# Up projection of a hybrid encoder layer: one matmul of 512 columns in place of two of 256, and sums of products kept in PSUM

## The chip, the cores and the metric

The kernel runs on one core of a Trainium2 chip. The metric is the time of one execution in microseconds; the comparison is by the median of several runs.

## What is computed

One layer of a bidirectional encoder on a sequence of 512 tokens with 2048 channels, in float32. Cut to what matters here:

```python
xn = rms_norm(x, attn_norm_g)
u_val, u_gate, q, k, v = split(xn @ w_in)            # 2048 -> 5120
y_conv = conformer_conv(u_val, u_gate, ...)          # width 31, layer norm, swish
y_na = neighborhood_attention(q, k, v, rpb)          # 16 heads, 8 x 64 grid
x = x + concat(rms_norm(y_conv), rms_norm(y_na)) @ w_out
xn = rms_norm(x, ffn_norm_g)
up = depthwise_conv(xn @ w_up, ffn_dw_w, ffn_dw_b)   # 2048 -> 11264, width 3
gate, val = split(up)
x = x + (silu(gate) * val) @ w_down                  # 5632 -> 2048
return rms_norm(x, final_norm_g)
```

## The kernel before

Every large matrix is used in two parts, so that matmuls in a fast float32 format give nearly full precision: a high part (`whi`, the value rounded to the format, made by ScalarE) and a low part (`wlo`, the rest, made by VectorE as a difference). A product is then three matmuls: high weights by high data, high weights by low data, low weights by high data (`mm3`, L126 to L128).

The stages follow one another: the input projection `project` (80 units of 8 x 3 matmuls of 512 columns, with convolution and attention beside it), the output projection `out_half` (two halves of 16 units), the up projection `up` and `hidden` (44 blocks f, each of 128 gate and 128 value columns), and the down projection (`product2`). The up and the down projection use a scheme for 2 x 2 blocks with seven products in place of eight, numbered c = 0 to 6. The weights of a product are a quarter of the matrix's block (A11, A12, A21, A22) or a sum of quarters: c = 0, 3 and 5 take A22, A11 and A12 as they are; c = 1 is A22 + A21, c = 2 is A21 + A11, c = 4 is the sum of 1 with A11, c = 6 the sum of 4 with A12. Signs are put into the data. `TURN` and `TURN2` are the orders of the products in the two projections.

Data of a product in the up projection: `comb[c][k]`, a tile of 128 x 512, whose left half holds the high parts of 256 combined token columns and whose right half the low parts.

Weights come by one list, `plan`: `weights()` takes the next entry, and has the entries up to 3 ahead (`AHEAD`) made. An entry made means: a load of 512 KB from HBM into one of seven `raw` buffers (`raw_unit`, on SyncE's queue, L110), then the split into `whi` and `wlo` (`parts`, L115 and L116), of which there are four buffers each. Sums of quarters begin earlier, up to 8 entries ahead (`FAR`), by the table `sums`. In the up projection the sums 1 and 2 are a load and a second transfer, on POOL's queue, that adds to the buffer (`summed`, L588); 4 and 6 are made by VectorE in the buffer of 1 (L595). For the down projection the sums are made in HBM ahead of time: a job copies a quarter to a scratch tensor `wsum[c][k]` (L176) and a second transfer adds another quarter to it (L177). There are 4 x 22 jobs. `sum_ahead` issues one behind a given matmul; it is called after certain units of the input and output projections, and after the fourth product of each block of the up projection.

The order of work on each engine is made by a scheduler from the order of the program and the dependencies; each engine then executes its own queue in that order, and POOL's and SyncE's queues issue the transfers. Of PSUM's eight banks, three have the tag "mm", one "po", two together "sc", and two "tr".

In a block of the up projection the products 3, 0, 1, 4, 5, 2, 6 go into four PSUM tiles of 256 columns. Products 4 and then 2 are added onto product 3, and product 6 onto product 1. ScalarE keeps copies in between (`kept`, L641), and VectorE adds (L648 to L650):

```python
a = kept(uu[:, 0], product(3))
kept(vv[:, 0], product(0))
b = kept(vv[:, 1], product(1))
kept(uu[:, 1], product(4, a))
add(g[:, 0], uu[:, 0], product(5))
add(v, vv, both(product(2, a)))
add(g[:, 1], uu[:, 1], product(6, b))
```

The rest of `hidden` scales, runs the width-3 convolution (L658 to L660), silu and the product with the gate, and writes the hidden row to HBM (the last 8 stay).

Of the kernel before, what the change touches and what calls it, by code (L numbers as in the profile page):

```python
# [10 lines left out]
F32 = mybir.dt.float32  # L11
F32R = mybir.dt.float32r
AF = mybir.ActivationFunctionType
ALU = mybir.AluOpType
# [20 lines left out]
U = 8  # L35
# [12 lines left out]
NW = 4  # L48
NEG = -1.0e30

TURN = (3, 0, 1, 4, 5, 2, 6)
TURN2 = (3, 0, 4, 1, 2, 6, 5)
Q = D // 2 // S
TAIL = 4
# [16 lines left out]
def layer(ctx: ExitStack, tc: tile.TileContext, xT, w_in, w_out, w_up, w_down, par, tab, g3, out):  # L71
# [36 lines left out]
    def raw_unit(src, n):  # L108
        raw = t4([P, U * P], "raw")
        return raw, nc.sync.dma_start(raw[:, :n], src)  # L110

    def parts(raw, n):
        hi = wpool.tile([P, U * P], F32R, tag="whi", name="whi", bufs=NW)
        lo = wpool.tile([P, U * P], F32R, tag="wlo", name="wlo", bufs=NW)
        i = nc.scalar.activation(hi[:, :n], raw[:, :n], AF.Copy)  # L115
        j = nc.vector.tensor_sub(lo[:, :n], raw[:, :n], hi[:, :n].bitcast(F32))  # L116
        return hi, lo, i, j

    def unit(src, n):

        return parts(raw_unit(src, n)[0], n)[:2]
# [37 lines left out]


    A11, A12, A21, A22 = range(4)
    wsum = {c: [dram.tile([P, U * P], F32, name=f"ws{c}_{k}") for k in range(NK)] for c in (1, 2, 4, 6)}
# [7 lines left out]
    def sum_ahead(ins):  # L170

        if not jobs:
            return
        c, k = jobs.pop(0)
        a, b = {1: (w_down[k, A22], A21), 2: (w_down[k, A21], A11), 4: (wsum[1][k], A11), 6: (wsum[4][k], A12)}[c]
        behind(nc.gpsimd.dma_start(wsum[c][k], a), ins)  # L176
        nc.gpsimd.dma_start(wsum[c][k], w_down[k, b], accum_op=ALU.add, max_dma_last_dim=ROW)  # L177

# [7 lines left out]
    def sum_sq(acc, src, first, to=slice(0, S)):  # L186
        if first:
            nc.scalar.activation(acc, src, AF.Square)
        else:
            q = t2("sq")[:, to]  # L190
            nc.scalar.activation(q, src, AF.Square)
            nc.vector.tensor_add(acc, acc, q)

    def rsqrt_steps(acc, n, name, to=slice(0, S), keep=True):

        m = (to.stop - to.start) // P
        ps = psa.tile([P, 2, S], F32, tag="sc", name="st")[:, 0]
# [16 lines left out]
        ps = psa.tile([P, 2, S], F32, tag="sc", name="st")[:, 0]  # L214
# [4 lines left out]
        nc.scalar.activation(res[:, to], ps[:, :m * P], AF.Copy)  # L219
        return res  # L220
# [51 lines left out]
    def project(n):  # L272
        ps = psm.tile([P, S], F32, tag="mm", name="pj")
        for u in range(KD // U):
            w = weights()
            for k in range(U):
                kk = u * U + k
                m = mm3(ps, w, k, xs[kk][0], xs[kk][1], kk == 0, kk == KD - 1)
            tick(m)
            if weights.at > 6 and weights.at % 2:  # L280
                sum_ahead(m)
            while late:
                late.pop()()
        return ps
# [292 lines left out]
    def stats2():  # L577
        rstd2.append((yield from rsqrt_steps(acc2, D, "rstd2")))

    def factors(f, at):  # L580

        def load(q):
            a[q] = raw_unit(w_up[f, q], U * P)[0]
            return a[q]

        def summed(c, q1, q2):
            a[c] = raw_unit(w_up[f, q1], U * P)[0]
            nc.gpsimd.dma_start(a[c], w_up[f, q2], accum_op=ALU.add)  # L588

        def make(c):  # L590
            if c in plain:
                return load(plain[c])
            if c in (1, 2):
                return a["s%d" % c]
            add(a["s1"], a["s1"], a[A11 if c == 4 else A12])  # L595
# [11 lines left out]
    order2 = [*range(NK - KEEP // 2, NK), *range(NK - KEEP // 2)]  # L607
    for c in TURN2:
        for k in order2:
            plan.append(lambda c=c, k=k: (unit(wsum[c][k] if c in wsum else w_down[k, {0: A22, 3: A11, 5: A12}[c]],  # L610
                                               U * P), operand(c, k)))

    out_half(mb, after)
    steps.append(stats2())

    def up(f, done):

        def product(c, onto=None):

            w = weights()  # L620
            ps = onto
            if ps is None:
                ps = (psa.tile([P, S], F32, tag="po", name="pu") if c == 1 else
                      psm.tile([P, S], F32, tag="mm", name="pu"))[:, :H]
            for k in range(U):
                m = comb[c][k]
# [3 lines left out]
            return ps  # L630

        def pair(name):
            return t2(name).rearrange("p (i t) -> p i t", i=2)

        def both(x):
            return x.unsqueeze(1).broadcast_to([P, 2, H])

        vv, uu, v, g = pair("vv"), pair("uu"), pair("vl"), pair("g")

        def kept(t, ps):  # L640
            nc.scalar.activation(t, ps, AF.Copy)  # L641
            return ps

        a = kept(uu[:, 0], product(3))
        kept(vv[:, 0], product(0))
        b = kept(vv[:, 1], product(1))
        kept(uu[:, 1], product(4, a))
        add(g[:, 0], uu[:, 0], product(5))  # L648
        add(v, vv, both(product(2, a)))
        add(g[:, 1], uu[:, 1], product(6, b))  # L650
        g, v = (t.rearrange("p i t -> p (i t)") for t in (g, v))
        return g, v

    def conv3(a, n):
# [24 lines left out]
    def operand(c, k):  # L679

        (b11, b12), (b21, b22) = ((hs[i][:, :H], hs[i][:, H:]) for i in (2 * k, 2 * k + 1))
        if c in (3, 5, 6):
            src = {3: b11, 5: b21, 6: b22}[c]
        else:
            t = t2("hc")
            src, m = t[:, :H], t[:, H:]
            if c == 2:
                nc.vector.tensor_sub(src, b22, b12)
            elif c == 1:
                nc.vector.tensor_sub(src, b11, b12)  # L690
# [7 lines left out]
        nc.vector.tensor_sub(t[:, H:], src, t[:, :H].bitcast(F32))  # L698
        return t
# [213 lines left out]
```

## Time and profile before

| | |
|---|---|
| time, median of 3 runs (lowest, highest) | 2038.44 us (2036.22, 2039.22) |
| the profiled execution's own time | 2037.69 us |
| its span | 2035.9 us |
| mean granted TensorE clock | 0.997 |
| TensorE matmuls, busy | 2005.8 us |
| VectorE, busy | 1593.5 us |
| ScalarE, busy | 1017.6 us |
| HBM read, written | 425.02 MB, 110.10 MB |

The span is from the first to the last instruction of one profiled execution. Matmuls are pipelined, so the duration of one (283 ns for 256 columns in the up projection) is longer than the step from one to the next. By the matmuls on each line, the input projection and the attention end near 505 us, the output projection near 708, the up projection runs from 708.1 to 1599.3, and the down projection from there to the end. DMA shares are the mean busy share of the 16 DMA engines; q1 carries the transfers issued by SyncE, q0 those issued by POOL.

### The profile page before, as it was taken

How to read it: one execution, taken by the hardware profiler on the slowest of the kernel's cores; microseconds unless marked ns; L12 is line 12 of the kernel's file. 1: busy time of each engine (PE TensorE's matmuls, PEld its weight loads, DVE VectorE, ACT ScalarE, POOL GpSimd, SP SyncE). 2: the span in 40 equal slices, each digit the busy share in tenths (PEclk: the TensorE clock that was granted, in tenths of full speed). 3: DMA queues.
4: the chain of work that ended last, by engine and by line, in shares of the span. 5: the costliest groups of instructions: out<-in, count | busy, mean ns of one | idle time of the engine just before them, and what ended most of it. 6: DMA issues, size and time to landing. Idle time of an engine off the chain costs nothing.

```text
span 2035.9 us, 32324 instructions
## 1 busy us (share of the span) xinstructions
PE 2005.8 (99%) x12620; PEld 1795.3 (88%) x12620; DVE 1593.5 (78%) x2223; ACT 1017.6 (50%) x1548; POOL 227.7 (11%) x314
## 2 busy tenths in 40 slices
PE   8999999999999999999999999999999999999997
PEld 6888888877787899999999999999999888888886
DVE  7985798497547878888888888888888698885764
ACT  6234423447525654545455555555455544554663
POOL 0111111011001111111111111111110300000000
PEclk9999999999999999999999999999999999999999
DMA  6676677677757889999999999999886976666563
GB/s 234 167 224 182 171 177 202 181 185 207 227 145 202 206 215 257 239 255 244 252 245 247 258 247 248 245 255 245 237 222 181 341 233 217 213 213 195 191 213 124
DMA packets 140873, 444.96 MB, mean 219 GB/s; under 512 B 15793, under 2 KB 23985, under 8 KB 139313
## 3 DMA queue, kind: packets, MB, share of 16 engines
q1 hardware_dynamic: 97776, 292.94, 42.5%
q0 software_dynamic: 42944, 149.97, 35.3%
q8 instruction: 99, 1.62, 0.3%
q14 instruction: 54, 0.43, 0.1%
HBM read 425.02 MB, written 110.10 MB: 263 GB/s over the span
## 4 chain that ended last, share of the span: by engine, by line
PE 76%; issue 21%; ACT 1%; DMA 1%; DVE 1%; POOL 0%; SPq 0%; POOLq 0%; DVEq 0%
PE pu L126 15%; PE pu L127 15%; PE pu L128 15%; PE pj L126 7%; PE pj L128 6%; PE pj L127 6%; PE po L126 3%; PE po L127 3%; PE po L128 3%; PE po L437 1%; PE sc L397 1%; PE trp L424 1%; DMA raw<-in_w_in 1%; DMA tab<-in_tab 0%; PE trx L537 0%
## 5 line engine op out<-in xcount | busy, mean ns | idle before, releaser
L115 ACT ACTIVATE whi<-raw 128x1024 fp32r<-128x1024 f32 x574 | 606.2, 1057 | 810.7 <-PE pj L127 219.3
L116 DVE TENSOR_TENSOR wlo<-raw,whi 128x1024 fp32r<-128x1024 f32 x574 | 700.7, 1222 | 265.2 <-ACT whi L115 230.4
L126 PE MATMUL pu<-xc,whi 128*128 128x256 f32 x2464 | 697.5, 283 | 1.3 <-ACT uu L641 1.3
L128 PE MATMUL pu<-xc,wlo 128*128 128x256 f32 x2464 | 697.9, 283 | 0.0
L127 PE MATMUL pu<-xc,whi 128*128 128x256 f32 x2464 | 697.7, 283 | 0.0
L126 PEld LDWEIGHTS pu<-xc,whi 128*128 128x128 f32 x2464 | 473.1, 192 | 2.0 <-ACT uu L641 1.7
L128 PEld LDWEIGHTS pu<-xc,wlo 128*128 128x128 f32 x2464 | 473.1, 192 | 0.2 <-issue 0.2
L127 PEld LDWEIGHTS pu<-xc,whi 128*128 128x128 f32 x2464 | 473.2, 192 | 0.1
L126 PE MATMUL pj<-xh,whi 128*128 128x512 f32 x640 | 254.0, 398 | 7.7 <-ACT whi L115 7.7
L128 PE MATMUL pj<-xh,wlo 128*128 128x512 f32 x640 | 251.0, 392 | 1.1 <-DVE wlo L116 1.1
L127 PE MATMUL pj<-xl,whi 128*128 128x512 f32 x640 | 251.3, 393 | 0.0
L737 PE MATMUL pd<-whi,ho 128*128 128x512 f32 x616 | 240.5, 391 | 2.2 <-DVE ho L698 2.2
L735 PE MATMUL pd<-whi,ho 128*128 128x512 f32 x616 | 240.5, 391 | 1.3 <-ACT ho L697 1.3
L736 PE MATMUL pd<-wlo,ho 128*128 128x512 f32 x616 | 240.6, 391 | 0.0
L311 DVE SCALAR_TENSOR_TENSOR y<-ch,prm,y 128x507 f32<-128x507 f32 (+14 forms) x240 | 169.7, 738 | 3.3
L126 PEld LDWEIGHTS pj<-xh,whi 128*128 128x128 f32 x640 | 120.8, 189 | 35.8 <-ACT whi L115 9.0
L128 PEld LDWEIGHTS pj<-xh,wlo 128*128 128x128 f32 x640 | 120.8, 189 | 28.6 <-DVE wlo L116 2.5
L127 PEld LDWEIGHTS pj<-xl,whi 128*128 128x128 f32 x640 | 120.9, 189 | 24.7 <-issue 0.7
L737 PEld LDWEIGHTS pd<-whi,ho 128*128 128x128 f32 x616 | 116.1, 188 | 27.1 <-DVE ho L698 3.0
L735 PEld LDWEIGHTS pd<-whi,ho 128*128 128x128 f32 x616 | 115.9, 188 | 25.7 <-ACT ho L697 1.5
L736 PEld LDWEIGHTS pd<-wlo,ho 128*128 128x128 f32 x616 | 116.0, 188 | 24.9 <-DVE wlo L116 0.6
L177 POOL DMA_DIRECT2D ws<-in_w_down x88 | 79.5, 904 | 360.5 <-DMA ws<-ws 185.1
(161 smaller groups left out, 2029.1 us busy)
## 6 DMA issues: line engine op xcount, KB each, us to landing
raw<-in_w_up SPq DMA_DIRECT2D x220, 512.0 KB, 5.8
ws<-in_w_down POOLq DMA_DIRECT2D x132, 512.0 KB, 7.3
raw<-in_w_up POOLq DMA_DIRECT2D x88, 512.0 KB, 7.9
raw<-ws SPq DMA_DIRECT2D x88, 512.0 KB, 4.2
raw<-in_w_in SPq DMA_DIRECT2D x80, 512.0 KB, 4.8
raw<-in_w_down SPq DMA_DIRECT2D x66, 512.0 KB, 4.0
ws<-ws POOLq DMA_DIRECT2D x44, 512.0 KB, 4.7
raw<-in_w_out SPq DMA_DIRECT2D x32, 512.0 KB, 4.7
```

Of the source, the lines that this page charges most:

```text
L115: i = nc.scalar.activation(hi[:, :n], raw[:, :n], AF.Copy)
L116: j = nc.vector.tensor_sub(lo[:, :n], raw[:, :n], hi[:, :n].bitcast(F32))
L126: nc.tensor.matmul(ps, hi[:, a], mh, start=start, stop=False, skip_group_check=more)
L127: nc.tensor.matmul(ps, hi[:, a], ml, start=False, stop=False, skip_group_check=more)
L128: return nc.tensor.matmul(ps, lo[:, a], mh, start=False, stop=stop, skip_group_check=more)
L177: nc.gpsimd.dma_start(wsum[c][k], w_down[k, b], accum_op=ALU.add, max_dma_last_dim=ROW)
L311: nc.vector.scalar_tensor_tensor(y[:, a:b], h[:, a + j - PAD:b + j - PAD], prm[:, o + j:o + j + 1], y[:, a:b], op0=ALU.mult, op1=ALU.add)
L397: m = nc.tensor.matmul(both[:, j, i, :], q[hp, b * P:(b + 1) * P], grid(k, KC0[b], KW)[hp], start=True, stop=True)
L424: m = nc.tensor.transpose(ps[:, 2 * i + ch, :], s[:, i, ch * P:(ch + 1) * P], ident)
L735: nc.tensor.matmul(ps[i], h[:, t], wh[:, d], start=start and not more, stop=False, skip_group_check=more)
L736: nc.tensor.matmul(ps[i], h[:, t], wl[:, d], start=False, stop=False, skip_group_check=more)
L737: return nc.tensor.matmul(ps[i], h[:, tl], wh[:, d], start=False, stop=stop, skip_group_check=more)
```

## The change

The up projection computes both products with the high weights by one matmul: high weights by the whole tile of 512 columns, whose left half is by the high data and whose right half by the low. The low weights follow by a matmul of 256 columns into the left half. A product thus fills a whole PSUM bank, and its value is the sum of the two halves; `folded` makes it (ScalarE copies the right half, VectorE adds the left). Where a product must be added to a sum that another product needs as well, ScalarE copies the bank into a second bank (`copied`), and the matmuls go on adding there. Three matmuls ahead of the up projection write the banks once. Six banks are held for the whole stage; the statistics use a "tr" bank there.

The weights of c = 4 get a `raw` buffer of their own (VectorE adds 1 and A11 into it), and after their split a transfer on POOL's queue adds A12 to it for c = 6. For the down projection the sums for c = 2 are no longer made in HBM: each is loaded and added to in a `raw` buffer, up to 8 entries ahead of its use. There remain 3 x 22 jobs, called at other units. The order of the products in a block becomes 3, 2, 4, 5, 1, 0, 6.

```diff
-TURN = (3, 0, 1, 4, 5, 2, 6)
+TURN = (3, 2, 4, 5, 1, 0, 6)
...
-    wsum = {... for c in (1, 2, 4, 6)}
-    jobs = [(c, k) for k in range(NK) for c in (1, 4, 2, 6)]
+    wsum = {... for c in (1, 4, 6)}
+    jobs = [(c, k) for k in range(NK) for c in (1, 4, 6)]
...
+    def stat():
+        if where:
+            return psa.tile([P, S], F32, tag="tr", name="st", bufs=2)
+        return psa.tile([P, 2, S], F32, tag="sc", name="st")[:, 0]
...
-            if weights.at > 6 and weights.at % 2:
+            if weights.at > 6 and weights.at % 3:
                 sum_ahead(m)
...
-            if d % 3 == 0:
+            if d % 2:
                 sum_ahead(i)
...
         def make(c):
             if c in plain:
                 return load(plain[c])
-            if c in (1, 2):
-                return a["s%d" % c]
-            add(a["s1"], a["s1"], a[A11 if c == 4 else A12])
-            return a["s1"]
+            if c == 4:
+                a[4] = t4([P, U * P], "ws")
+                add(a[4], a[1], a["q", A11])
+            return a[4 if c == 6 else c]
+
+        def split_of(c):
+            w = parts(make(c), U * P)[:2]
+            if c == 4:
+                nc.gpsimd.dma_start(a[4], w_up[f, A12], accum_op=ALU.add)
+            return w
...
-        for c, qs in ((1, (A22, A21)), (2, (A21, A11))):
-            sums[at + TURN.index(c)] = lambda c=c, qs=qs: summed("s%d" % c, *qs)
-        return [lambda c=c: parts(make(c), U * P)[:2] for c in TURN]
+        sums[at + TURN.index(2)] = lambda: summed(2, A21, A11)
+        sums[at + TURN.index(4)] = lambda: summed(1, A22, A21)
+        return [lambda c=c: split_of(c) for c in TURN]
...
+    def summed2(k):
+        third[k] = raw_unit(w_down[k, A21], U * P)[0]
+        nc.gpsimd.dma_start(third[k], w_down[k, A11], accum_op=ALU.add)
+
+    def unit2(c, k):
+        if c == 2:
+            return parts(third[k], U * P)[:2]
+        return unit(...)
+
     for c in TURN2:
         for k in order2:
+            if c == 2:
+                sums[len(plan)] = lambda k=k: summed2(k)
...
+    ea = psa.tile([P, 2, S], F32, tag="sc", name="pu")
+    pd_, pb, pc_ = (psm.tile([P, S], F32, tag="mm", name="pu") for _ in range(3))
+    pe, pa = ea[:, 0], ea[:, 1]
+    for x in (pe, pd_, pb):
+        nc.tensor.matmul(x, comb[3][0][:, :P], comb[3][0], start=True, stop=True)
...
-                i = mm3(ps, w, k, m[:, :H], m[:, H:], k == 0 and onto is None, k == U - 1, onto is not None)
+                nc.tensor.matmul(ps, hi[:, w], m, start=k == 0 and not more, stop=False, skip_group_check=more)
+                i = nc.tensor.matmul(ps[:, :H], lo[:, w], m[:, :H], start=False, stop=k == U - 1,
+                                     skip_group_check=more)
...
+        def copied(to, ps):
+            nc.scalar.activation(to, ps, AF.Copy)
+
+        def folded(to, ps):
+            nc.scalar.activation(to, ps[..., H:], AF.Copy)
+            add(to, to, ps[..., :H])
+
+        product(3, pa, False)
+        copied(pd_, pa)
+        product(2, pc_, False)
+        w = t2("w")[:, :H]
+        folded(w, pc_)
+        product(4, pa, True)
+        copied(pe, pa)
+        product(5, pd_, True)
+        g = t2("g")
+        folded(g[:, :H], pd_)
+        product(1, pa, True)
+        copied(pb, pa)
+        product(0, pe, True)
+        v = t2("vl")
+        by = v.rearrange("p (i t) -> p i t", i=2)
+        folded(by, ea)
+        add(by, by, w.unsqueeze(1).broadcast_to([P, 2, H]))
+        product(6, pb, True)
+        folded(g[:, H:], pb)
```

More of the change, by code (lines that the diff above doesn't have):

```diff
@@ L161, in layer @@
     A11, A12, A21, A22 = range(4)
-    wsum = {c: [dram.tile([P, U * P], F32, name=f"ws{c}_{k}") for k in range(NK)] for c in (1, 2, 4, 6)}
-    jobs = [(c, k) for k in range(NK) for c in (1, 4, 2, 6)]
+    wsum = {c: [dram.tile([P, U * P], F32, name=f"ws{c}_{k}") for k in range(NK)] for c in (1, 4, 6)}
+    jobs = [(c, k) for k in range(NK) for c in (1, 4, 6)]
     def behind(i, ins):
@@ L174, in sum_ahead @@
         c, k = jobs.pop(0)
-        a, b = {1: (w_down[k, A22], A21), 2: (w_down[k, A21], A11), 4: (wsum[1][k], A11), 6: (wsum[4][k], A12)}[c]
+        a, b = {1: (w_down[k, A22], A21), 4: (wsum[1][k], A11), 6: (wsum[4][k], A12)}[c]
         behind(nc.gpsimd.dma_start(wsum[c][k], a), ins)
@@ L192, in sum_sq @@
             nc.vector.tensor_add(acc, acc, q)
+    def stat():
+        if where:
+            return psa.tile([P, S], F32, tag="tr", name="st", bufs=2)
+        return psa.tile([P, 2, S], F32, tag="sc", name="st")[:, 0]
+    where = []
     def rsqrt_steps(acc, n, name, to=slice(0, S), keep=True):
         m = (to.stop - to.start) // P
[L197 removed]
+        ps = stat()
         for i in range(m):
@@ L582, in load @@
         def load(q):
-            a[q] = raw_unit(w_up[f, q], U * P)[0]
-            return a[q]
+            a["q", q] = raw_unit(w_up[f, q], U * P)[0]
+            return a["q", q]
         def summed(c, q1, q2):
@@ L607, in layer @@
     order2 = [*range(NK - KEEP // 2, NK), *range(NK - KEEP // 2)]
+    third = {}
+    def summed2(k):
[4 more added lines that the diff above has]
+            return parts(third[k], U * P)[:2]
+        return unit(wsum[c][k] if c in wsum else w_down[k, {0: A22, 3: A11, 5: A12}[c]], U * P)
     for c in TURN2:
         for k in order2:
-            plan.append(lambda c=c, k=k: (unit(wsum[c][k] if c in wsum else w_down[k, {0: A22, 3: A11, 5: A12}[c]],
-                                               U * P), operand(c, k)))
+            if c == 2:
+                sums[len(plan)] = lambda k=k: summed2(k)
+            plan.append(lambda c=c, k=k: (unit2(c, k), operand(c, k)))
@@ L613, in layer @@
     out_half(mb, after)
+    where.append(1)
     steps.append(stats2())
-    def up(f, done):
[L618 to L624, printed above, removed]
+    ea = psa.tile([P, 2, S], F32, tag="sc", name="pu")
+    pd_, pb, pc_ = (psm.tile([P, S], F32, tag="mm", name="pu") for _ in range(3))
@@ L628, in product @@
             tick(i)
             done(TURN.index(c), i)
[L630 to L651, printed above, removed]
+        def copied(to, ps):
[5 more added lines that the diff above has]
+        copied(pd_, pa)
```

6 lines of the change are left out of this document (4 added, 2 removed).

## The prediction

> **What bounds the kernel now.** I read the page first: parts 1 and 2 for the engine that is never idle, part 4 for the chain, part 5 for the groups that the change touches.
>
> ```profile
> span 2035.9 us, 32324 instructions
> PE 2005.8 (99%) x12620; PEld 1795.3 (88%) x12620; DVE 1593.5 (78%) x2223; ACT 1017.6 (50%) x1548; POOL 227.7 (11%) x314
> PE 76%; issue 21%; ACT 1%; DMA 1%; DVE 1%; POOL 0%; SPq 0%; POOLq 0%; DVEq 0%
> L115 ACT ACTIVATE whi<-raw 128x1024 fp32r<-128x1024 f32 x574 | 606.2, 1057 | 810.7 <-PE pj L127 219.3
> L116 DVE TENSOR_TENSOR wlo<-raw,whi 128x1024 fp32r<-128x1024 f32 x574 | 700.7, 1222 | 265.2 <-ACT whi L115 230.4
> L126 PE MATMUL pu<-xc,whi 128*128 128x256 f32 x2464 | 697.5, 283 | 1.3 <-ACT uu L641 1.3
> L128 PE MATMUL pu<-xc,wlo 128*128 128x256 f32 x2464 | 697.9, 283 | 0.0
> L127 PE MATMUL pu<-xc,whi 128*128 128x256 f32 x2464 | 697.7, 283 | 0.0
> raw<-in_w_up SPq DMA_DIRECT2D x220, 512.0 KB, 5.8
> raw<-in_w_up POOLq DMA_DIRECT2D x88, 512.0 KB, 7.9
> ```
>
> TensorE is busy for 99% of the span, and the chain of waits is TensorE or TensorE's own issue. The three groups of the up projection (pu) have 2464 matmuls each and waited 1.3 us in all of it: that stage is a solid row of matmuls. So next I asked what else is nearly full there, with the busy time by stretches.
>
> ```profile
> core 0: us, PE busy (x) PEld busy (x) DVE busy (x) ACT busy (x) POOL busy (x), PEclk, DMA share, GB/s
> 1030.00:1130.00 100.00, 100.00 (x836) 100.00 (x835) 83.26 (x94) 51.60 (x70) 15.36 (x20) 1.00 0.96 248
> 1520.00:1570.00 50.00, 50.00 (x419) 50.00 (x419) 42.26 (x49) 27.55 (x38) 3.47 (x4) 1.00 0.65 173
> 1800.00:1900.00 100.00, 100.00 (x443) 82.82 (x442) 64.49 (x91) 47.16 (x66) 0.00 (x0) 1.00 0.64 205
> ```
>
> The DMA engines are at 0.96 while the sums of w_down (the jobs) run in the up projection, at 0.65 there when they have ended, and at 0.64 in the down projection. TensorE sets the time; DMA is second, and the change moves work onto it.
>
> **The matmuls: minus 32.9 us.** A product of the up projection is 8 blocks of three matmuls of 256 columns; it becomes 8 blocks of one of 512 (high weights, both halves of the data) and one of 256 (low weights). Columns stay 6144 and one instruction of three goes, so the gain is what an instruction costs beside its columns. The timeline of TensorE has both sizes: 256 columns in the up projection, 512 in the down projection, first and last row of a stretch of each.
>
> ```profile
> 1000.11 0.28 PE L127 MATMUL pu<-xc,whi 128*128 128x256 f32 x1
> 1011.99 0.28 PE L127 MATMUL pu<-xc,whi 128*128 128x256 f32 x1
> ...
> 1719.87 0.39 PE L735 MATMUL pd<-whi,ho 128*128 128x512 f32 x1
> 1723.95 0.39 PE L735 MATMUL pd<-whi,ho 128*128 128x512 f32 x1
> ```
>
> Between the first two lie 99 steps: 11.88 / 99 = 120.0 ns. Between the last two lie 18: 4.08 / 18 = 226.7 ns. The second 256 columns cost 106.7 ns, so each matmul carries 13.3 ns of its own. A product goes from 24 x 120.0 = 2.880 us to 8 x (226.7 + 120.0) = 2.773 us; 2464 / 8 = 308 products save 308 x 0.107 = 32.9 us. Sizes in turn are in no row; I take the mean of the two steps, since each step covers the load of one set of 128 columns in both rows. A block f of seven products then lasts 19.4 us instead of 20.2.
>
> The page TensorE: Matmul & The Clock Gate of the Trainium skill (Back-to-back issue gap) gives columns / 2.4 + 2.5 ns, so only 2.5 ns go with each removed matmul. By it the gain would be 308 x 8 x 2.5 = 6.2 us. The trace says 13.3 ns, at full clock, and decides.
>
> **DMA in the up projection: nothing.** Jobs fall from 88 to 66 (c = 2 is gone). Their places: units 7 to 80 of the input projection not divisible by three, 50; every second of the 2 x 16 units of the output projection, 16; together 66. So none is left for the up projection, where the new third sum per block takes their room. Prices per transfer come from the queues in a stretch after the last job:
>
> ```profile
> q1 hardware_dynamic: 2181, 7.93, 39.6%
> q0 software_dynamic: 703, 2.55, 23.8%
> ```
>
> The stretch is 60 us. Plain loads: 0.396 x 60 / 7.93 = 3.00 us of all 16 engines per MB, 1.57 us for 512 KB (0.524 MB). Adding transfers: 0.238 x 60 / 2.55 = 5.60 per MB, 2.94 for 512 KB. A block has five loads (7.9), the write of the hidden row (0.262 MB, 0.8) and now three sums (8.8): 17.5 us in 19.4, 0.90, below the 0.96 at which TensorE did not wait.
>
> **The c = 2 pass of the down projection: plus 19 us.** Its 22 weights were loaded ready from wsum. Now each is loaded and a second one added: 1.57 + 2.94 = 4.51 us of DMA for a unit that TensorE does in 12 x 0.2267 = 2.72 us. The pass asks 22 x 4.51 = 99 us of DMA in 59.8. Lead must make up the rest. How far loads run ahead:
>
> ```profile
> 1602.17 0.60 PE L737 MATMUL pd<-whi,ho 128*128 128x512 f32 x1 [0.56 <-DVE ho L698]
> 1700.71 5.76 SPq L110 DMA_DIRECT2D raw<-ws  x3
> 1075.00:1080.00 5.00, 5.00 (x44) 5.00 (x43) 4.78 (x7) 3.52 (x5) 0.89 (x1) 1.00 1.07 262
> ```
>
> The third pass starts some 44 x 2.72 us after 1602, near 1722, and its first load is issued at 1700.7: 21 us, 7.7 units ahead. The sums are ordered five units earlier (8 against 3), so at most 34.7 us ahead. In these, at a DMA share between 0.96 and the 1.07 of the fullest five microseconds (third row), 33 to 37 us are served; five ordinary loads take 7.9, which leaves 25 to 29, 5.6 to 6.5 units, and the seven raw buffers allow about that. The other 15.5 to 16.4 units need 70 to 74, over the same shares 65 to 77 us, with 3 us for the xr loads in between; the last must also land (7.9 less its 2.94) and be split (1.06 + 1.22), some 7 us. TensorE wants it 57.1 us into the pass. Stall: 65 + 7 - 57 = 15 to 77 + 3 + 7 - 57 = 30. I take 19, nearer the low end, since the high end adds every part in a row; 0 stays the end if transfers overlap better than any row shows.
>
> **The job chain on POOL: nothing, up to 20 us.** Jobs 4 and 6 of one k each copy the sum that the job before wrote; until now a job on c = 2 lay between.
>
> ```profile
> 51.75 0.66 POOL L176 DMA_DIRECT2D ws<-in_w_down  x1 [50.45 <-PE pj L128]
> 297.75 0.91 POOL L177 DMA_DIRECT2D ws<-in_w_down  x1 [4.59 <-DMA ws<-in_w_down]
> 305.23 0.51 POOL L176 DMA_DIRECT2D ws<-ws  x1 [6.57 <-DMA ws<-in_w_down]
> 309.54 0.90 POOL L177 DMA_DIRECT2D ws<-in_w_down  x1 [3.81 <-DMA ws<-ws]
> 495.38 0.51 POOL L176 DMA_DIRECT2D ws<-in_w_down  x1 [6.95 <-PE pj L128]
> ```
>
> Copy to sum 4.3 us, sum to the next copy 7.5: 11.8 for a job that follows its own sum, 5.2 for the first of a k, 28.8 for three. The units' pace is (495.38 - 51.75) / 72 = 6.16 us, so 4.5 units 27.7: POOL falls behind by 1.1 us per k over 17, some 19 us, and catches up in the output projection, where three jobs get 6 units. Only if landings slow by a microsecond does it reach the up projection late, and the first sums of w_up stand behind it on POOL's queue; that costs up to 20 us once. Both ends are kept; I take zero.
>
> **PSUM copies and folds: plus 4 us.** Four copies to SBUF become three from bank to bank, four folds and their adds:
>
> ```profile
> L641 ACT ACTIVATE uu<-pu x88: 356/363/368, 722.3 to 1592.2; 128x256 f32<-128x256 f32 x88
> L648 DVE TENSOR_TENSOR g<-uu,pu x44: 408/420/424, 724.2 to 1602.0; 128x256 f32<-128x256 f32 x44
> L649 DVE TENSOR_TENSOR vl<-vv,pu x44: 679/686/689, 731.2 to 1602.4; 128x512 f32<-128x512 f32 x44
> L219 ACT ACTIVATE rstd<-st x2: 597/598/600, 42.8 to 724.5; 128x512 f32<-128x512 f32 x2
> ```
>
> ScalarE per block: 3 x 0.6 + 3 x 0.36 + 0.6 = 3.5 us where 1.5 stood; it was at 51.6 of 100 us, 10.4 a block, so 12.4 of 19.4. VectorE: three adds of 0.42 and two of 0.69 for two and one, plus 1.1; one sum of 1024 columns less, minus 1.2. Neither is full. What counts is slack. A copy out of pa must end within the one product that follows, 2.77 us: 0.6 and little else, hidden unless ScalarE is held. The fold of ea before product 3 writes pa again is the tight one: 0.28 (the last matmul) + 0.60 + 0.69 = 1.6 us, and with one split in front on each engine (1.06, 1.22) 3.9. So 0 to 1.1 us per block, 0 to 48 us. Waits of the kind in the trace:
>
> ```profile
> ACT whi L115 <- DVE raw L595: 170.2, 85, 3.2
> PE pu L126 <- ACT uu L641: 1.3, 1, 1.3
> ```
>
> ScalarE did stand up to 3.2 us behind VectorE, yet TensorE waited for it once. I take 0.1 us a block, 4 us.
>
> **Start of the up projection: plus 2 us.** Three matmuls that fill the banks (0.7 us) and a wait until all three "mm" banks are read, about a fold (1.1); at most 4.
>
> **The sum** is made on the profiled execution, 2037.69 us (span 2035.9): 2037.69 - 32.9 + 19 + 4 + 2 = 2029.8. The median of the runs, 2038.44, lies 0.75 above it, so 2030.5.
>
> **Rivals.** First, the down projection hides its sums: the lead suffices or the sums come cheaper. For it: DMA stands at 0.64 there. Against: 99 us asked in 59.8. It gives 2030.5 - 19 = 2011.
>
> Second, slower: the ring of raw buffers closes into a loop in every block. The tile of a[4] makes six buffers a block out of seven, and its add waits for the sum a[1]; if the loads behind it wait for that add, the loop is add 1.2, three issues 1.0, load 5.8, landing 7.9, 15.9 us, and one to two sums of 2.94 queued in front make 18.8 to 21.8. It decides above 19.4: at 20.4 a block loses 1 us, 44 blocks 44 us, 2074; half of it 2052. For it: four queue waits in a row, and a third sum. Against: TensorE never waited on the same loads at a DMA share of 0.96. The ea fold, at 0.5 us a block, looks alike in time (2030.5 - 4 + 22 = 2048), but its wait would end with VectorE.
>
> Third, the job chain reaches the up projection late: 2030.5 + 20 = 2050. Fourth, the change doesn't do what it says: alternating sizes keep a cost per block and only 6.2 us go: 2030.5 + 32.9 - 6.2 = 2057. The page TensorE: Matmul & The Clock Gate of the Trainium skill (Back-to-back issue gap) would come to that time.
>
> **How the numbers follow.** Chances: the forecast 0.45 (own range 2023 to 2040), the first rival 0.10, the second with the ea fold 0.30 (2038 to 2074), the third 0.10, the fourth 0.05. A measurement of this kernel can tell 0.2%, 4 us, from no change. Faster: the first rival and 0.38 of the forecast, 0.48. Same, 2034.4 to 2042.5: 0.07 of the forecast and 0.04 of the second, 0.11. Slower: 0.41. Leaving out some 0.08 below and 0.12 above, the range is 2013 to 2058.
>
> **What would show it.** Right: in the up projection 16 matmuls of a product in 2.77 us, with no idle time in the 44 blocks; no w_down transfer there; a DMA share near 0.9; between the fifth pass's first and last matmul some 79 us instead of 59.8, TensorE's waits there ending with the split of a third tile, and the DMA share at 1. Wrong: waits of TensorE for whi or ea inside blocks, POOL still on jobs after the up projection's start, or a fifth pass of 60 us.

## The result, and the profile after

| | before | after |
|---|---|---|
| time, median (lowest, highest) | 2038.58 us (2036.22, 2039.22) | 2212.17 us (2209.49, 2218.79) |
| ratio, 95% interval | | 1.0859 [1.0832, 1.0886] |
| span of the profiled execution | 2035.9 us | 2208.5 us |
| start of the up projection (first pu matmul of a block) | 708.1 us | 771.0 us |
| up projection, first to last matmul | 891.3 us | 989.6 us |
| behind it | 436.5 us | 447.9 us |

The change costs 172.6 us of span: 62.9 ahead of the up projection, 98.3 in it, 11.4 behind it. The page of the changed kernel, span, engines, chain and the two groups of up-projection matmuls:

```profile
span 2208.5 us, 27706 instructions
PE 2028.1 (92%) x10159; PEld 1665.7 (75%) x10159; DVE 1570.8 (71%) x2267; ACT 1090.2 (49%) x1680; POOL 252.3 (11%) x336
PE 69%; DMA 12%; issue 9%; ACT 8%; DVE 1%; POOL 0%; SPq 0%; POOLq 0%; ACTq 0%; DVEq 0%
L654 PE MATMUL pu<-xc,whi 128*128 128x512 f32 x2464 | 886.9, 403 | 82.1 <-ACT whi L115 44.2
L655 PE MATMUL pu<-xc,wlo 128*128 128x256 f32 x2464 | 678.1, 281 | 0.0
```

The solid row of matmuls is gone: TensorE is busy for 92% where 99% stood, and DMA and ScalarE are in the chain of waits. Four stretches of the changed kernel follow (columns as in the prediction): two ahead of the up projection, one in its blocks, one in the down projection.

```profile
615.00:710.00 95.00, 60.12 (x279) 47.97 (x277) 43.40 (x80) 35.20 (x64) 12.66 (x18) 0.84 0.73 175
710.00:730.00 20.00, 0.00 (x0) 0.00 (x0) 0.00 (x0) 0.00 (x0) 4.72 (x6) 0.50 0.77 151
830.00:1630.00 800.00, 737.27 (x4035) 617.13 (x4034) 583.14 (x721) 436.63 (x612) 94.16 (x108) 1.00 0.78 201
2000.00:2100.00 100.00, 89.94 (x377) 69.33 (x376) 52.73 (x61) 41.58 (x62) 14.80 (x17) 1.00 0.95 263
```

At 710 to 730 us TensorE, VectorE and ScalarE do nothing at all and POOL alone issues transfers. In the blocks TensorE is busy for 92%, and the DMA share is 0.78, below the 0.96 at which TensorE did not wait in the kernel before. So it is not the DMA engines that are full there. The gap ahead of the up projection, from TensorE's list of waits, VectorE's timeline and then POOL's:

```profile
PE trx L544 <- DVE x L555: 58.9, 1, 58.9
730.78 1.23 DVE L602 TENSOR_TENSOR ws<-raw 128x1024 f32<-128x1024 f32 x1 [59.36 <-DMA raw<-in_w_up]
733.24 0.69 DVE L555 TENSOR_TENSOR x<-x,oa 128x512 f32<-128x512 f32 x1
```

```profile
84.35 0.82 POOL L176 DMA_DIRECT2D ws<-in_w_down  x1
...
488.03 0.83 POOL L176 DMA_DIRECT2D ws<-in_w_down  x1
...
629.46 0.89 POOL L177 DMA_DIRECT2D ws<-in_w_down  x1 [4.23 <-DMA ws<-ws]
630.04 0.80 POOL L176 DMA_DIRECT2D ws<-in_w_down  x1
638.76 0.91 POOL L177 DMA_DIRECT2D ws<-in_w_down  x1 [7.92 <-DMA ws<-in_w_down]
...
662.01 0.81 POOL L176 DMA_DIRECT2D ws<-in_w_down  x1
...
711.58 0.99 POOL L595 DMA_DIRECT2D raw<-in_w_up  x1
...
722.78 0.90 POOL L595 DMA_DIRECT2D raw<-in_w_up  x1
```

VectorE stood 59 us at block 0's add of a[4] (L602). The output projection's own work (L555) stood behind it in VectorE's queue, and TensorE stood 58.9 us for that. The add waits for the sum a[1], which POOL issued only at 722.78, behind late jobs: the three jobs of one k took 662.01 - 630.04 = 32.0 us there. In the input projection, from 84.35 to 488.03 us, twelve k took 33.6 us each.

In nearly every block TensorE waits at the same two places, here 9.6 us apart, once for a copy of ScalarE (L661) and once for a split:

```profile
1011.54 0.50 PE L654 MATMUL pu<-xc,whi 128*128 128x512 f32 x1 [0.72 <-ACT pu L661]
1021.16 0.98 PE L654 MATMUL pu<-xc,whi 128*128 128x512 f32 x2 [1.03 <-ACT whi L115]
```

A block lasts 22.3 us where TensorE's work is 19.4 by the prediction. (In this document a block's length is the step from one hidden row's product to the next, averaged from the third block on.)

### The profile page after: what moved, and what is told of

Its sections match the earlier page's. It is cut to its first block, busy times and chain, and to the rows that moved or that the text cites. A ratio compares the mean times of both kernels' runs of the same rounds, so it can differ in the third digit from the quotient of the medians.

```text
span 2208.5 us, 27706 instructions
## 1 busy us (share of the span) xinstructions
PE 2028.1 (92%) x10159; PEld 1665.7 (75%) x10159; DVE 1570.8 (71%) x2267; ACT 1090.2 (49%) x1680; POOL 252.3 (11%) x336
## 4 chain that ended last, share of the span: by engine, by line
PE 69%; DMA 12%; issue 9%; ACT 8%; DVE 1%; POOL 0%; SPq 0%; POOLq 0%; ACTq 0%; DVEq 0%
PE pu L654 25%; PE pu L655 11%; PE pj L126 6%; PE pj L128 6%; PE pj L127 6%; DMA ws<-in_w_down 6%; PE pd L771 4%; PE pd L770 4%; PE pd L769 4%; ACT whi L115 3%; ACT uy L692 3%; DMA ws<-ws 3%; DMA raw<-in_w_down 2%; ACT pu L661 1%; DMA raw<-in_w_up 1%
## 5 line engine op out<-in xcount | busy, mean ns | idle before, releaser
L654 PE MATMUL pu<-xc,whi 128*128 128x512 f32 x2464 | 886.9, 403 | 82.1 <-ACT whi L115 44.2
L115 ACT ACTIVATE whi<-raw 128x1024 fp32r<-128x1024 f32 x486 | 513.0, 1057 | 744.5 <-PE pu L654 257.4
L116 DVE TENSOR_TENSOR wlo<-raw,whi 128x1024 fp32r<-128x1024 f32 x486 | 592.6, 1221 | 304.1 <-ACT whi L115 282.2
L655 PE MATMUL pu<-xc,wlo 128*128 128x256 f32 x2464 | 678.1, 281 | 0.0
L654 PEld LDWEIGHTS pu<-xc,whi 128*128 128x128 f32 x2464 | 463.6, 188 | 225.3 <-ACT pu L661 59.1
L655 PEld LDWEIGHTS pu<-xc,wlo 128*128 128x128 f32 x2464 | 466.4, 189 | 4.2 <-issue 0.2
L116 DVE TENSOR_TENSOR wlo<-ws,whi 128x1024 fp32r<-128x1024 f32 x88 | 107.4, 1220 | 150.4 <-ACT whi L115 150.4
L115 ACT ACTIVATE whi<-ws 128x1024 fp32r<-128x1024 f32 x88 | 93.4, 1061 | 158.6 <-PE pu L654 153.8
L595 POOL DMA_DIRECT2D raw<-in_w_up x88 | 77.8, 884 | 737.1 <-DMA raw<-in_w_up 468.6
L770 PEld LDWEIGHTS pd<-wlo,ho 128*128 128x128 f32 x616 | 115.6, 188 | 38.3 <-DVE wlo L116 14.9
```

Source lines behind the costliest of these rows:

```text
L654: nc.tensor.matmul(ps, hi[:, w], m, start=k == 0 and not more, stop=False, skip_group_check=more)
L655: i = nc.tensor.matmul(ps[:, :H], lo[:, w], m[:, :H], start=False, stop=k == U - 1, skip_group_check=more)
L770: nc.tensor.matmul(ps[i], h[:, t], wl[:, d], start=False, stop=False, skip_group_check=more)
```

## The experiments

Four theories are tested. In them "the add" is VectorE's addition into a[4] (L602), and "the sum" is the adding transfer on POOL's queue that completes a[1] (L595).

- A, the shared tile: pe and pa are the two banks of one tile, `ea`, so a matmul into one waits for the reader of the other. TensorE's order and ScalarE's copies then set the length of a block.
- B, the second rival of the prediction: a loop of add, load, sum and next add sets it.
- C: the jobs, late on POOL's queue, make the gap ahead of the up projection.
- D: the c = 2 pass of the down projection costs what its additions cost.

The numbers in parentheses behind a heading are the ratio to the kernel before and its 95% interval.

**1. Tiles of their own** (1.0738 [1.0694, 1.0781]). The up projection holds five PSUM banks (two of `ea`, three with the tag "mm"), not six, so the "po" bank is free there, and pa moves to it.

```diff
-    pe, pa = ea[:, 0], ea[:, 1]
+    pe, pa = ea[:, 0], psa.tile([P, S], F32, tag="po", name="pa")
...
-        folded(by, ea)
+        folded(by[:, 1], pa)
+        folded(by[:, 0], pe)
```

> Edit: the banks pe and pa become two tiles (pa takes the "po" bank), and the fold of both is done in two parts; nothing else. Theory A (shared tile): the copy of pa and product 0 on pe wait for each other because both banks are one tile; the scheduler fills that wait with one matmul of the next block's product 2, whose weights are not split yet. Then both waits of a block (1.03 us for whi, 0.72 for a copy, some 2.75 us with what follows them) go: the up projection falls from 989.6 to 860 to 875 us, the time from 2212 to some 2090. Theory B (loop of raw buffers and sums, the second rival of the prediction): a block stays at 22 us and the time above 2195.

2186.38 us: only 26 less, where A expected 2090. TensorE's wait for whi is gone, yet a block lasts 21.8 us. The timeline (VectorE, SyncE's queue, POOL) shows a loop:

```profile
1004.40 1.22 DVE L602 TENSOR_TENSOR ws<-raw 128x1024 f32<-128x1024 f32 x1 [1.99 <-issue]
...
1013.14 1.21 DVE L116 TENSOR_TENSOR wlo<-raw,whi 128x1024 fp32r<-128x1024 f32 x1
1014.38 0.33 SPq L110 DMA_DIRECT2D raw<-in_w_up  x1
1020.87 0.86 POOL L595 DMA_DIRECT2D raw<-in_w_up  x1 [8.44 <-DMA raw<-in_w_up]
1026.52 1.22 DVE L602 TENSOR_TENSOR ws<-raw 128x1024 f32<-128x1024 f32 x1 [3.49 <-DMA raw<-in_w_up]
```

From the add VectorE works without a pause for 10.0 us, to the wlo (1013.14 + 1.21) that frees a raw buffer; the load into it is issued at once, takes 6.5 us, the sum on it 5.7, and the next add starts: 22.1 us.

**2. TensorE's order kept as written, the tile still shared** (1.0897 [1.0851, 1.0944])

```diff
-                nc.tensor.matmul(ps, hi[:, w], m, ...)
-                i = nc.tensor.matmul(ps[:, :H], lo[:, w], m[:, :H], ...)
+                pin(nc.tensor.matmul(ps, hi[:, w], m, ...))
+                i = pin(nc.tensor.matmul(ps[:, :H], lo[:, w], m[:, :H], ...))
```

> Edit: the matmuls of the up projection keep the order of the program; tiles as in the changed kernel. Theory A: no matmul of product 2 stands early any more, so the wait for whi goes (1.8 us a block), but product 0 now waits openly for the copy of pa, 0.28 + 0.6 + some 0.1, about 1 us a block: up projection 905 to 930 us, time near 2140. Theory B: no change, above 2195.

2221.8 us, a block of 22.4: no gain, where A expected 2140. The wait for whi went here too, but TensorE waits for the copies for longer (32.3 us in the changed kernel). So the order alone is not the price of the shared tile:

```profile
PE pu L654 <- ACT pu L661: 69.7, 55, 1.5
```

**3. The jobs paced as before** (1.0763 [1.0747, 1.0779])

```diff
-            if weights.at > 6 and weights.at % 3:
+            if weights.at > 6 and weights.at % 2:
...
-            if d % 2:
+            if d % 3 == 0:
```

> Edit: the jobs are called at the units of the kernel before (odd units of the input projection, every third of the output projection), so 49 of 66 are issued before the up projection and 17 inside it. Theory C: the gap of 59 us before the up projection is POOL's queue, late with the jobs, and VectorE standing at the first block's add behind it. Then the gap goes: up projection starts near 710 instead of 771, time near 2152. Rival: the gap is the wait for w_up's own sums and stays, time 2205 to 2215, or the 17 jobs slow the first 17 blocks by 1 us or more each and give 20 us back.

2195.24 us. The up projection starts at 709.3 us, so the gap is gone, as C says. But 18 jobs now run in it, and it takes 1035.7 us, 46 more, 2.6 a job. While they run TensorE is busy for 84% (830 to 1100 us), behind them for 92% (1200 to 1700 us).

**4. The second addend of c = 2 left out** (1.0767 [1.074, 1.0794]). The output lacks that part.

```diff
-        nc.gpsimd.dma_start(third[k], w_down[k, A11], accum_op=ALU.add)
+        pass
```

> Edit: in the down projection the c = 2 weights are loaded but the second quarter is not added (22 transfers of 512 KB on POOL's queue left out; the output lacks that part). Theory D: the c = 2 pass is held by the DMA engines, 4.5 us asked in 2.72 a unit; without the sums its waits go, 10 to 12 us, time near 2201. Rival: these waits have another cause and the time stays within 3 us of 2212.

2192.91 us. The matmuls of the down projection, before, after and here:

```profile
L735 PE MATMUL pd<-whi,ho x616: 388/389/628, 1600.9 to 2024.2; 128*128 128x512 f32 x154
```

```profile
L769 PE MATMUL pd<-whi,ho x616: 387/389/497, 1762.5 to 2197.1; 128*128 128x512 f32 x154
```

```profile
L769 PE MATMUL pd<-whi,ho x616: 387/389/499, 1756.1 to 2175.8; 128*128 128x512 f32 x154
```

From the first to the last of these matmuls 434.6 us fall to 419.7, so the additions cost 14.9 us; against the kernel before (423.3) the stage lost 11.3. D holds for the stage. The whole run is 19 us shorter than the changed kernel: its down projection also starts 6.4 us earlier (1756.1 against 1762.5), which the edit does not explain.

**5. Jobs of two k side by side** (1.0493 [1.0474, 1.0512])

```diff
-    jobs = [(c, k) for k in range(NK) for c in (1, 4, 6)]
+    jobs = [(c, k) for p in range(0, NK, 2) for c in (1, 4, 6) for k in (p, p + 1)]
```

> The changed kernel with the order of the jobs alone changed: two k side by side, so that between a job's load with its first addition and the copy that stores the sum stands the same job of the next k. Theory C (in the changed kernel the jobs' chain on GpSimd's queue, 32.0 us per k in the trace because each copy waits for the addition just ahead of it, runs late into the start of the up projection and holds up the first weights' sums by 59 us): the copies find their sums landed, the gap of 59 us at 671 to 731 us goes or falls under 10 us, the up projection starts at 708 to 715 us and still takes 985 to 990 us; time 2212 - 55 = 2150 to 2165 us. Rival (the gap comes from the transfers' load in the attention, not from the order of the jobs): the start stays at 765 us or later and the time over 2200 us.

2138.03 us, 74 less. No job waits for the sum just ahead of it any more. The stretch in which TensorE lost 35 us is full at a DMA share of 0.93, and the up projection starts at 706.9:

```profile
615.00:710.00 95.00, 94.92 (x447) 76.17 (x446) 77.24 (x142) 61.03 (x113) 15.85 (x21) 1.00 0.93 224
```

C is shown. Its blocks still last 22.3 us.

**6 and 7. One sum left out, on either side of the add** (both with tiles of their own; the output lacks that part)

```diff
-            nc.gpsimd.dma_start(a[c], w_up[f, q2], accum_op=ALU.add)
+            if c != 1:                                     # run 6
+                nc.gpsimd.dma_start(a[c], w_up[f, q2], accum_op=ALU.add)
...
-            if c == 4:                                     # run 7
-                nc.gpsimd.dma_start(a[4], w_up[f, A12], accum_op=ALU.add)
```

> The kernel with pe and pa in tiles of their own, and the sum a[1] = A22 + A21 left out: A22 alone is loaded (32 additions of 512 KB less; the hidden part is another one). Loop theory (VectorE's addition of a[4], then its queue up to the wlo that frees a raw buffer, then the load, then the sum on it, then the next addition: 22.1 us in the trace of the kernel with tiles of their own): the 5.7 us of the sum fall out of the loop, the next limit is TensorE's work or GpSimd's other sum, and a block falls to 19.4 to 20.0 us, the up projection to 855 to 885 us, the time to 2186 - 85 to 115 = 2070 to 2100 us. DMA theory (the transfers' sum sets the block): one accumulation of three is gone, a block falls by up to 2.9 us to 19.4 us as well; the next run, with another accumulation of the same size left out, tells the two apart. Copies theory (ScalarE's copies between PSUM banks set the block): it stays at 21.5 to 22.1 us.

> The kernel with pe and pa in tiles of their own, and the addition of A12 onto a[4] left out: the same number of bytes and the same kind of transfer less per block as in the run without the sum on a[1], but behind VectorE's addition of a[4] and not ahead of it. Loop theory: the addition of a[4] still waits for the load and the sum of a[1], a block stays at 21.5 to 22.1 us, the time within 2150 to 2190 us. DMA theory: a block falls as far as in the run without the sum on a[1].

2086.66 us (1.0249 [1.0184, 1.0315]) and 2192.23 us (1.075 [1.071, 1.079]). A block is 19.5 us without the sum ahead of the add and 21.8 without the one behind it, though a transfer of the same size and kind is left out. The stretch 830 to 1600 us, run 6 and then run 7:

```profile
830.00:1600.00 770.00, 770.00 (x4444) 673.05 (x4443) 645.66 (x837) 484.55 (x715) 68.74 (x79) 1.00 0.73 201
```

```profile
830.00:1600.00 770.00, 718.00 (x3952) 617.64 (x3951) 572.17 (x740) 425.98 (x636) 60.90 (x70) 0.97 0.65 181
```

Run 7 has the lower DMA share and loses the time: latency in a loop, not bandwidth. B is shown for the kernel with separate tiles. In run 6, where that loop is open, TensorE is busy in every microsecond of the stretch, so ScalarE's copies between banks cost it nothing there.

**8. Eight raw buffers for seven** (with tiles of their own; 1.1568 [1.1545, 1.1592])

```diff
-NT = 79
-NR = 7
+NT = 77
+NR = 8
```

> The kernel with pe and pa in tiles of their own, and eight raw buffers in place of seven (two [128, 512] tiles less). Loop theory: the load of A22 for the sum on a[1] takes a buffer that was freed one unit earlier, and no longer waits for the last wlo of VectorE's queue behind the addition; per block of seven units that is about 3 us earlier, the wait of VectorE for the sum goes, a block falls to 19.4 to 20.5 us, the time to 2065 to 2120 us. DMA theory and copies theory: a block stays at 21.5 to 22.1 us and the time within 1% of 2186 us.

2359.38 us, worse by 173 than run 1, a block of 25.8 us, where B expected 19.4 to 20.5. The edit does two things, since room for the eighth buffer comes from two fewer of the 79 small tiles. The granted clock was lower as well, 0.90 from 830 to 1600 us against 0.98 in run 1. What either adds is not separated. The rows of its timeline:

```profile
1202.77 1.23 DVE L602 TENSOR_TENSOR ws<-raw 128x1024 f32<-128x1024 f32 x1 [5.01 <-DMA raw<-in_w_up]
...
1213.01 0.68 DVE L708 TENSOR_TENSOR uy<-uy 128x512 f32<-128x512 f32 x1
1213.72 0.33 SPq L710 DMA_DIRECT2D h<-uy  x1
1214.89 0.33 SPq L110 DMA_DIRECT2D raw<-in_w_up  x1
1221.42 0.86 POOL L595 DMA_DIRECT2D raw<-in_w_up  x1 [7.60 <-ACT g L664]
1229.45 1.23 DVE L602 TENSOR_TENSOR ws<-raw 128x1024 f32<-128x1024 f32 x1 [4.64 <-DMA raw<-in_w_up]
```

The loop is still there and has another way through: the write of the hidden row, which waits for the end of VectorE's queue, stands in SyncE's queue right in front of the load, and the sum takes 8.0 us in place of 5.7. The Trainium skill says (Perfetto Trace Analysis, Optimization Strategy) that the same bubble repeated on the engine that should be full can mean too few buffers. Here one buffer more, with two small tiles fewer, made the block longer, 25.8 us against 21.8. What shortened it, with seven buffers, was another place for the add in VectorE's queue (runs 11 and 12). Why the sum takes 2.4 us more here stays open.

**9 to 12. The add behind the wlo of product 2**, alone, and with the other two edits. `parts` returns that wlo as its last value:

```diff
-                add(a[4], a[1], a["q", A11])
+                with tc.issue_after(a["lo"].ins):
+                    add(a[4], a[1], a["q", A11])
...
-            w = parts(make(c), U * P)[:2]
+            w = parts(make(c), U * P)
+            a["lo"], w = w[3], w[:2]
```

Alone:

> The changed kernel with one thing moved: VectorE's addition of a[4] may stand only behind the wlo of the product before it (the unit of product 2), where it stands in the text of the kernel, and not five wlo earlier, where the list of the queue now has it. Nothing is added or taken out. Loop theory (addition, VectorE's queue behind it, the load of A22 into the buffer that this queue frees, the sum, the next addition): the sum gets a block's time, the wait goes, a block falls from 22.3 to 19.4 to 20.5 us (at the upper end if the shared tile of pe and pa keeps a wait of its own), the up projection from 989.6 to 860 to 905 us; at its start VectorE no longer stands ahead of the attention's last work, of the gap of 59 us 25 to 59 us go too; time 2212 - 110 to 190 = 2020 to 2100 us. Rival (the two-bank tile and the copies set the block): a block stays at 21.5 us or more and the time over 2150 us.

With the interleaved jobs:

> The interleaved order of the jobs and the later addition together, pe and pa still in one two-bank tile. If the two causes are apart and sum up: 2138 us (measured with the interleaved order alone) less what the later addition saves in the 44 blocks (2.0 to 2.9 us each, 88 to 127 us), 2010 to 2050 us. The difference to the next run is the price of the shared tile: 0 if its wait is only where the loop's delay shows, some 40 us (0.98 us a block) if it is a cost of its own.

With both, the interleaved jobs and the tiles of their own:

> Interleaved jobs, later addition, and pe and pa in tiles of their own. With the loop and the late jobs gone, a block is TensorE's own 19.4 us as in the run without the sum on a[1]: up projection 707 to 1563 us, the last pass over c = 2 still 11 to 15 us dearer than before: 2037 - 33 + 13 = 2017 us, 2010 to 2030 us, faster than the kernel before by 0.3% to 1.3%. Rival (the price of ScalarE's copies between banks, hidden so far behind the loop, appears): a block at 20.0 us or more, 2040 us or more.

With the tiles of their own and the jobs as changed:

> Tiles of their own for pe and pa and the later addition, with the jobs in the changed kernel's order: the fourth corner, which prices the jobs' chain where nothing else waits. In the run with the later addition alone the up projection began at 746 us in place of 771, so of the gap some 35 to 40 us should be left; block 19.5 us as with all three. Time 2016.7 + 35 to 60 = 2052 to 2077 us. If the chain costs nothing once the addition stands later: 2017 to 2025 us.

| tiles | jobs | add | time, us | ratio to before | block, us |
|---|---|---|---|---|---|
| shared | changed | early | 2212.17 | 1.0859 [1.0832, 1.0886] | 22.3 |
| shared | interleaved | early | 2138.03 | 1.0493 [1.0474, 1.0512] | 22.3 |
| own | changed | early | 2186.38 | 1.0738 [1.0694, 1.0781] | 21.8 |
| shared | changed | late | 2216.14 | 1.0863 [1.0819, 1.0908] | 22.4 |
| shared | interleaved | late | 2142.96 | 1.0513 [1.0496, 1.0529] | 22.4 |
| own | changed | late | 2089.54 | 1.0253 [1.0236, 1.027] | 19.6 |
| own | interleaved | late | 2016.72 | 0.9892 [0.9877, 0.9908] | 19.5 |

The later add alone gains nothing: B is not the only cause. Separate tiles alone gain 26 us. With the add late, separate tiles gain 127 and 126 us; with the tiles separate, the later add gains 97. So two limits of 21.8 to 22.4 us lie over each other, and either one hides the removal of the other. In the changed kernel itself the shared tile's is the longer one: from 830 to 1630 us, 36 blocks, the add hardly waited, and never for the sum:

```profile
DVE ws L602 <- DVE g L703: 1.0, 3, 0.5
```

The shared tile's limit, from the kernel of the fifth row, TensorE's matmuls and weight loads and ScalarE:

```profile
1005.50 0.50 PE L656 MATMUL pu<-xc,whi 128*128 128x512 f32 x1 [0.78 <-ACT pu L663]
1013.96 0.28 PE L657 MATMUL pu<-xc,wlo 128*128 128x256 f32 x1
1015.27 0.98 PE L656 MATMUL pu<-xc,whi 128*128 128x512 f32 x2 [1.03 <-ACT whi L115]
1005.50 0.19 PEld L656 LDWEIGHTS pu<-xc,whi 128*128 128x128 f32 x1 [1.09 <-ACT pu L663]
1015.27 0.19 PEld L656 LDWEIGHTS pu<-xc,whi 128*128 128x128 f32 x1 [1.35 <-ACT whi L115]
1015.75 0.19 PEld L656 LDWEIGHTS pu<-xc,whi 128*128 128x128 f32 x1 [0.30 <-ACT pu L663]
1003.47 0.80 ACT L694 ACTIVATE uy<-g,prm 128x512 f32<-128x512 f32 x1
1004.17 0.80 ACT L694 ACTIVATE uy<-vl,prm,fwn 128x512 f32<-128x512 f32 x1
1004.88 0.57 ACT L663 ACTIVATE pu<-pu 128x512 f32<-128x512 f32 x1
1014.16 1.06 ACT L115 ACTIVATE whi<-raw 128x1024 fp32r<-128x1024 f32 x1 [1.49 <-PE pu L656]
```

Here VectorE never waits for the sum. The waits of the weight loads add up to 1.09 + 1.35 + 0.30 = 2.7 us, nearly all of 22.4 - 19.5.

The first is at the start of product 4, which adds onto pa and must wait until ScalarE has copied pa. ScalarE did a split and two scalings (L694) first and began that copy only at 1004.88. Also, three of the sixteen matmuls of product 2, which stands between the products 3 and 4, had been moved ahead of product 3, so less work was left to cover the copy. The third (0.30) is product 0's wait for the copy out of pa. The second comes of TensorE's queue, whose order around one block's end is this (changed kernel; the program's list, not the trace):

```
L655 Matmult pu_6094<-xc_6085,wlo_11315 128x256
L654 Matmult pu_6097<-xc_5168,whi_11406 128x512 [waits DVE_49,Activation_49]
L654 Matmult pu_6094<-xc_5180,whi_11339 128x512 [waits Activation_49]
```

The first line ends product 1 and the third begins product 0, both in the shared tile (pu_6094). Product 0 must wait for the copy out of pa, and the scheduler put one matmul of the next block's product 2 in front of it. That matmul's whi uses the buffer that product 1 holds to its end (four buffers, four units back: 1, 0, 6, 3, 2). ScalarE therefore starts the split (1014.16) 0.2 us after the start of product 1's last matmul (1013.96), and TensorE stands until it is done (1015.27).

The job chain costs 74, 73 and 73 us in the three pairs that differ in the jobs alone. With the add late, VectorE no longer carries it; ScalarE does, in two waits for w_up sums that stand behind jobs (tiles of their own, jobs as changed, add late):

```profile
727.64 1.06 ACT L115 ACTIVATE whi<-raw 128x1024 fp32r<-128x1024 f32 x1 [33.01 <-DMA raw<-in_w_up]
...
797.03 1.06 ACT L115 ACTIVATE whi<-ws 128x1024 fp32r<-128x1024 f32 x1 [36.94 <-DMA ws<-in_w_up]
```

The kernel with all three edits beats the one before by 1.1%. Its page with the group of matmuls into pu (four of the seven products; the other three now go into the tile named pa), and a stretch of blocks:

```profile
span 2014.6 us, 27613 instructions
PE 1976.6 (98%) x10159; PEld 1654.2 (82%) x10159; DVE 1576.3 (78%) x2311; ACT 1099.4 (55%) x1724; POOL 253.0 (13%) x336
PE 90%; issue 4%; DMA 3%; ACT 1%; DVE 1%; POOL 1%; SPq 0%; POOLq 0%; ACTq 0%; DVEq 0%
L656 PE MATMUL pu<-xc,whi 128*128 128x512 f32 x1408 | 494.6, 393 | 0.0
```

```profile
800.00:1500.00 700.00, 700.00 (x4040) 612.16 (x4039) 588.37 (x757) 444.75 (x649) 95.11 (x108) 1.00 0.90 230
```

The up projection runs from 708.5 us to 1566.4, 857.9 us, 33.4 less than before; it starts 0.4 later, and what follows takes 11.7 more: -21.3 us, as the spans say (2014.6 against 2035.9).

## Why the prediction was wrong, step by step

2030.5 us (2013 to 2058) against 2212.17: the sign was wrong. The terms for the matmuls and for the c = 2 pass were near. What failed were two waits that it priced at next to nothing: those inside the blocks (4 us taken, 2138.03 - 2016.72 = 121 found) and those behind the job chain (0 taken, 2212.17 - 2138.03 = 74 found).

- Matmuls, -32.9: right, but visible only with the other limits gone. There the up projection is 33.4 us shorter, and a pair takes 857.9 us / 2464 = 348.2 ns against the 346.7 of the prediction. So the 13.3 ns of an instruction go, and the fourth rival falls. The 6.2 us gain by the Trainium skill's figure (TensorE: Matmul & The Clock Gate, Back-to-back issue gap) falls with it: the page gives that figure for an isolated matmul, and here each of the 10159 matmuls (PE) has a weight load (PEld) of its own.
- DMA in the up projection, nothing: right. A share of 0.90 was forecast, and with the three edits it is 0.90 beside a TensorE that is never idle.
- c = 2 pass, +19: the mechanism was right, the size was 11.3 against the kernel before, of which the additions cost 14.9. The first rival, that it is hidden, falls.
- Copies and folds, +4: as work they cost nothing once the waits are gone. The steps that failed are "hidden unless ScalarE is held", for a copy out of pa, and "The fold of ea before product 3 writes pa again is the tight one", priced at 0 to 1.1 us a block. The prediction took TensorE's order as written and each bank by itself. ScalarE was held, by a split and two scalings (1.09 us of waiting a block); and since the two banks are one tile, product 0 waited for a reader of pa (0.30), and the scheduler put a matmul in between whose weights were not split (1.35). The tile's price is 2.9 us a block, 126 us.
- The second rival had the right loop and the wrong sum. Its "three issues 1.0" stood where VectorE's queue behind the add takes 10.0 us; load and sum, 6.5 and 5.7, were a little under the 5.8 + 7.9 assumed. It gave 18.8 to 21.8 us, with 19.4 as the point from which it decides, and 22.1 came, in the kernel with separate tiles; in the changed kernel the shared tile's limit lay over it. "TensorE never waited on the same loads" did not carry over: it was read from a kernel without this loop.
- Job chain, "nothing, up to 20 us", and the third rival with it: the place was right, the size was not, and two steps failed. The first job of a k was given 5.2 us from copy to sum; queued right behind the last k's sum it took 638.76 - 630.04 = 8.7 (8.9 in the mean of the input projection, where the later copies took 5.0 in place of 4.3). So a k took 33.6 us in the input projection and not 28.8, against a pace of 27.7, and POOL fell behind by 5.9 us per k and not by 1.1. And the price of being late is not the lateness of one sum: an engine that waits in order keeps all that stands behind it waiting, 73 us.
- Start of the up projection, +2: with the three edits it starts 0.4 us later than before.
- What would show it: two of the signs listed as wrong are in the profile, waits for whi in the blocks and POOL on jobs past the start.

## What to carry to other kernels

Before a step is given zero because its engine is not full, write down the loop that it closes: each queue in order, with everything that stands in it behind the waiting instruction, then compare the loop with the stage's pace. When the fix for a wait that the trace shows moves nothing, look for a second limit of the same length before dropping the cause; here one fix gave 1.2%, another nothing, and both together 5.5%. Give banks that are read and written at different times tiles of their own, even where they are neighbours.

## What the runs showed of the hardware that was not expected

On POOL's queue the copy issued 0.6 us after an adding transfer (630.04 behind 629.46) let its own sum start only 8.7 us after its issue. This is no single case: from 80 to 500 us of the changed kernel 13 such copies took 6.8 to 11.7 us, 8.9 in the mean. In the kernel before, 16 copies of the same kind with nothing just ahead of them took 4.2 to 6.4, 4.6 in the mean, at nearly the same DMA share (0.71 against 0.74). What the copy waits for in that time stays open. Adding 512 KB from HBM took 5.7 us in one kernel and 8.0 in another. And the DMA share did not tell which kernel was short of data: at 0.90 over 700 us TensorE was never idle, at 0.65 it was idle for 7% of the time.
